# Prefix log-sum-exp on one core: the steps of a tile in another order, and the two-block tiles in other places

## The chip, the cores and the metric

The kernel runs on 1 core of one Trainium2 chip. The metric is the device time of one execution in microseconds, lower is better; the time of a kernel is the median of its runs. A separate, profiled execution left a trace: every instruction of every engine with its start and duration, and the transfers. Engine names in the profile: PE is TensorE (PEld its weight loads), DVE is VectorE, ACT is ScalarE, POOL is GpSimd, SP is SyncE, whose queue issues all of this kernel's transfers.

## The reference

```python
B, S, D = (4, 4096, 4128)           # x: float32, standard normal
out[:, 0, :] = x[:, 0, :].copy()
for t in range(1, S):
    mx = np.maximum(out[:, t - 1, :], x[:, t, :])
    out[:, t, :] = mx + np.log(np.exp(out[:, t - 1, :] - mx) + np.exp(x[:, t, :] - mx))
```

For each batch and column, row t of the output is the logarithm of the sum of exp(x) over rows 0 to t: a prefix sum between an Exp and a Ln.

## The kernel before, in words

**Tiles.** A batch has 4096 rows, 32 blocks of 128. A tile (`Step`) is r = 2 or 3 blocks: partition p of the tile holds r consecutive rows of all 4128 columns, so a tile is 128 x r x 4128 float32 (4128 KB or 6192 KB). A batch is cut into twelve tiles of [2, 3, 3, 3, 2, 3, 3, 3, 2, 3, 3, 2] blocks; four batches give 48 tiles (`steps`), 32 of three blocks and 16 of two. Four tile buffers rotate: one (`x2`) of two blocks, for tiles whose number in the batch divides by four, and three (`x3`) of three blocks. Exp, sums and Ln are done in place, so the output is stored from the buffer that the input was loaded into.

**Chunks.** The 4128 columns are cut into NC = 3 chunks of 1376 columns (`Chunk`). Each chunk of each tile goes through these steps:

- `exp` (L92, ScalarE): Exp of the chunk's r blocks, one instruction.
- `sums` (L94 to L107, VectorE): adds the r values of each partition. With r = 3, L103 puts block 0 + block 1 into block 1; L105 then writes the total into `z[c]`, on partitions 0 to 126 only. Partition 127 of `z[c]` still holds the running sum at the end of the previous tile, the carry.
- `head` (L113, TensorE): a product with a 128x128 matrix of ones and zeros gives, in a PSUM tile `pt` (two buffers), for each partition the sum of all earlier partitions and the carry (`carried`; in a batch's first tile `below`, without the carry). The profile shows six matmul records for each head.
- `add` (L117 to L130, VectorE): L121 adds `pt` to the first r - 1 blocks in place; L122 writes the sum of the last two blocks, the inclusive prefix at the partition's last row, into all of `z[c]`.
- `log` (L135 and L136, ScalarE): Ln of the first r - 1 blocks in place, and Ln of `z[c]` into the last block.

The next tile's L105 for the same chunk overwrites `z[c]`, so it must follow this L136.

**Probes.** The kernel takes Exp without subtracting a maximum. It records whether that was safe: the minimum over row 0 of a batch (L99, one partition, in `sums` of a batch's first tile) and the sum of `z` over the columns (L128, partitions 96 to 127, in `add` of a batch's last tile). At the end L188 to L202 turn these into a flag; if it is set, a slow general version runs (`_general`, not taken with these inputs).

**Order.** Nothing is scheduled by a planner: `manual_schedule()` leaves each engine with its instructions in the order in which the Python code writes them. The loop of before goes over all 144 chunks as one sequence, across tile borders. At chunk g it writes Exp of chunk g+2, sums of g+1, add of g, Ln of g, and then the head of g+1. With the last tile's chunks (`late`), Exp of g+2 and sums of g+1 come behind add and Ln of g.

**Transfers.** When the last chunk of a tile is done, SP gets the store of this tile i and behind it the load of tile i+3. That load goes into the buffer that tile i-1 used, so SP waits for the store of i-1 to have completed.

Of the kernel before, what the change touches and what calls it, by code (L numbers as in the profile page):

```python
# [10 lines left out]
ALU = mybir.AluOpType  # L11
AX = mybir.AxisListType
P = 128
MM = 512
NC = 3
# [5 lines left out]
def kernel(  # L21
# [5 lines left out]
    nc = tc.nc  # L27
    B, S, D = x.shape
# [16 lines left out]
        out=below, in_=below, pattern=[[1, P]], compare_op=ALU.is_ge,  # L45
# [5 lines left out]
        out=carried, in_=below, pattern=[[0, P]], compare_op=ALU.not_equal,  # L51
# [5 lines left out]
    probe = consts.tile([P, 2, B * NC], FP32, name="probe")  # L57
# [27 lines left out]
    class Chunk:  # L85
# [6 lines left out]
            nc.scalar.activation(e, e, ACT.Exp)  # L92

        def sums(self):  # L94
            t, r = self.t, self.t.r
            e = [t.xt[:, j, self.cols] for j in range(r)]
            if t.first:
                k = t.b * NC + self.c
                nc.vector.tensor_reduce(  # L99
                    out=probe[0:1, 1, k:k + 1], in_=e[0][0:1], op=ALU.min, axis=AX.X,  # L100
                )
            if r == 3:
                nc.vector.tensor_tensor(out=e[1], in0=e[0], in1=e[1], op=ALU.add)  # L103
            n = P - 1
            nc.vector.tensor_tensor(  # L105
                out=self.z[0:n], in0=e[r - 2][0:n], in1=e[r - 1][0:n], op=ALU.add,
            )  # L107
# [8 lines left out]

        def add(self):  # L117
            t, r = self.t, self.t.r
            e = t.xt[:, 0:r - 1, self.cols]
            base = self.pt.unsqueeze(1).to_broadcast([P, r - 1, CH])  # L120
            nc.vector.tensor_tensor(out=e, in0=base, in1=e, op=ALU.add)  # L121
            nc.vector.tensor_tensor(  # L122
                out=self.z, in0=t.xt[:, r - 2, self.cols], in1=t.xt[:, r - 1, self.cols],
                op=ALU.add,
            )
            if t.last:
                k = t.b * NC + self.c
                nc.vector.tensor_reduce(  # L128
                    out=probe[96:P, 0, k:k + 1], in_=self.z[96:P], op=ALU.add, axis=AX.X,
                )  # L130

        def log(self):
            t, r = self.t, self.t.r
            e = t.xt[:, 0:r - 1, self.cols]
            nc.scalar.activation(e, e, ACT.Ln)  # L135
            nc.scalar.activation(t.xt[:, r - 1, self.cols], self.z, ACT.Ln)  # L136

    steps = []
    for b in range(B):
        n = S // P  # L140
        parts = []
        while n:
            r = min(2 if len(parts) % 4 == 0 else 3, n)
            if n - r == 1:
                r = 2
            parts.append(r)
            n -= r
        assert len(parts) % 4 == 0 and min(parts) > 1
        row = 0
        for i, r in enumerate(parts):  # L150
            steps.append(Step(b, row, r, x3 if i % 4 else x2, i + 1 == len(parts)))
            row += P * r
        assert row == S

    chunks = [Chunk(s, c) for s in steps for c in range(NC)]
    bufs, ahead, stored = 4, 3, 0
    for s in steps[:bufs]:
        s.load()
    chunks[0].exp()
    chunks[1].exp()  # L160
    chunks[0].sums()
    chunks[0].head()
    n = len(chunks)
    for g, k in enumerate(chunks):
        nxt = chunks[g + 1] if g + 1 < n else None
        far = chunks[g + 2] if g + 2 < n else None
        late = far is None or far.t is steps[-1]
        if not late:
            far.exp()
            nxt.sums()  # L170
        k.add()
        k.log()
        if late:
            if far:
                far.exp()
            if nxt:
                nxt.sums()
        if k.c == NC - 1:
            k.t.store()
            if bufs <= stored + ahead < len(steps):  # L180
                steps[stored + ahead].load()
            stored += 1
        if nxt:
            nxt.head()


    bad = consts.tile([P, 2, B * NC], FP32, name="bad")
# [1 line left out]
        out=bad[:, 0, :], in0=probe[:, 0, :], scalar1=LARGE, scalar2=None, op0=ALU.is_le,  # L189
    )  # L190
    nc.vector.tensor_scalar(
        out=bad[:, 1, :], in0=probe[:, 1, :], scalar1=SMALL, scalar2=None, op0=ALU.is_ge,
# [3 lines left out]
        out=low, in_=bad.rearrange("p a k -> p (a k)"), op=ALU.min, axis=AX.X,  # L196
# [5 lines left out]
        out=flag, in0=good, scalar1=float(P), scalar2=None, op0=ALU.is_lt,  # L202
# [68 lines left out]
```

## Time and profile before

| | |
|---|---|
| median of 3 runs | 1296.87 us (1295.33 to 1296.93) |
| the profiled execution's own time | 1293.67 us |
| its span, first to last instruction | 1291.9 us |
| PE busy | 605.4 us, 47% |
| DVE busy | 996.0 us, 77% |
| ACT busy | 937.3 us, 73% |
| bytes moved | 541.28 MB, half read, half written |
| mean rate over the span | 419 GB/s |
| load of a three-block tile, issue to landing (median) | 38.9 us |
| store of a three-block tile, issue to landing (median) | 23.8 us |

How to read it: the shares of busy time are means over the whole span. The page also gives the span in 40 equal slices, one digit each (9 is 90% or more busy). A row of instructions says start, duration, engine, line, operation, output <- input with shapes, and in brackets the idle time ahead of it and what ended that. On one engine an instruction may start shortly before the listed end of the one in front of it, so "start to start" is the measure of what an instruction takes out of an engine's time.

### The profile page before, as it was taken

The page shows a single profiled execution, that of the slowest core. Times are in us where ns is not written, and L with a number is a line of the kernel's source. Part 1 is how long each engine was busy: PE and PEld are TensorE (multiplying, and loading weights), DVE is VectorE, ACT ScalarE, POOL GpSimd, SP SyncE. Part 2 cuts the span into 40 slices and gives each one's busy share as a digit, 9 for nine tenths or more (in the row PEclk, how much of TensorE's full clock was granted, in tenths as well). Part 3 has the DMA queues.
Part 4 walks back from the last instruction along what each step waited for, and adds up shares of the span by engine and source line. Part 5 has one row for each costly group of instructions (what it writes and reads, how often), then busy time and mean ns, then how long its engine had stood idle before and what let it go on. Part 6 is the DMA issues. An engine that isn't in the chain of part 4 may idle for free. (4 is left out here: it accounts for less than half of the span.)

```text
span 1291.9 us, 3364 instructions
## 1 busy us (share of the span) xinstructions
PE 605.4 (47%) x866; PEld 236.8 (18%) x866; DVE 996.0 (77%) x556; ACT 937.3 (73%) x433; POOL 4.6 (0%) x12
## 2 busy tenths in 40 slices
PE   2554356345555335545534534535534553463432
PEld 1221122112122112112211211211211221121110
DVE  4996798679689579669968957957968976895763
ACT  4996687678589669569669957866858866895761
POOL 1000000000000000000000000000000000000000
PEclk9766666667567667666766766766776666676566
DMA  9999999999999999999999999999999999999964
GB/s 402 423 413 428 433 429 432 436 430 404 438 433 427 439 427 431 435 430 420 423 425 435 439 428 439 428 438 426 415 429 429 435 434 432 434 437 429 433 279 180
DMA packets 13843, 541.28 MB, mean 419 GB/s; under 512 B 1536, under 2 KB 1536, under 8 KB 1536
## 3 DMA queue, kind: packets, MB, share of 16 engines
q1 hardware_dynamic: 13824, 541.07, 97.6%
q8 instruction: 7, 0.11, 0.0%
q14 instruction: 12, 0.10, 0.0%
HBM read 270.53 MB, written 270.53 MB: 419 GB/s over the span
## 5 line engine op out<-in xcount | busy, mean ns | idle before, releaser
L113 PE MATMUL pt<-z,carried 128*128 128x512 f32 (+1 forms) x792 | 557.9, 867 | 613.2 <-DVE z L105 613.2
L92 ACT ACTIVATE xt<-xt 128x4128 f32<-128x4128 f32 (+1 forms) x144 | 467.7, 3249 | 240.3 <-DMA xt<-in_x_dram 240.3
L113 PEld LDWEIGHTS pt<-z,carried 128*128 128x128 f32 x792 | 218.0, 293 | 952.4 <-issue 952.4
L121 DVE TENSOR_TENSOR xt<-pt,xt 128x2752 f32<-128x2752 f32 (+1 forms) x144 | 365.6, 2539 | 20.9 <-PE pt L113 20.9
L135 ACT ACTIVATE xt<-xt 128x2752 f32<-128x2752 f32 (+1 forms) x144 | 303.8, 2109 | 100.3 <-DVE z L122 99.7
L103 DVE TENSOR_TENSOR xt<-xt 128x1376 f32<-128x1376 f32 x96 | 152.3, 1587 | 216.4 <-ACT xt L92 216.3
L105 DVE TENSOR_TENSOR z<-xt 127x1376 f32<-127x1376 f32 x144 | 228.9, 1590 | 17.8 <-ACT xt L92 13.8
L122 DVE TENSOR_TENSOR z<-xt 128x1376 f32<-128x1376 f32 x144 | 229.3, 1593 | 4.9
L136 ACT ACTIVATE xt<-z 128x1376 f32<-128x1376 f32 x144 | 192.0, 1333 | 0.0
L113 PE MATMUL pt<-z,below 128*128 128x512 f32 (+1 forms) x72 | 47.3, 817 | 54.4 <-DVE z L105 54.4
L99 DVE TENSOR_REDUCE probe<-xt 1x1 f32<-1x1376 f32 x12 | 18.9, 1571 | 21.8 <-ACT xt L92 21.7
L113 PEld LDWEIGHTS pt<-z,below 128*128 128x128 f32 x72 | 18.7, 276 | 83.1 <-issue 82.9
L128 DVE TENSOR_REDUCE probe<-z 32x1 f32<-32x1376 f32 x12 | 19.0, 1581 | 0.4
L62 POOL MEMSET z<- 128x1376 f32 x3 | 3.7, 1245 | 0.0
L199 PE MATMUL good<-ones,low 128*1 128x1 f32 x2 | 0.2, 164 | 5.4 <-DVE low L195 5.4
L33 ACT ACT_TABLE_LOAD x1 | 1.3, 1283 | 0.8 <-PEq L255 0.8
L199 PEld LDWEIGHTS good<-ones,low 128*1 128x1 f32 x2 | 0.1, 82 | 6.0 <-DVE low L195 6.0
L201 DVE TENSOR_SCALAR flag<-good 1x1 int32<-1x1 f32 x1 | 0.1, 147 | 0.3 <-PE good L199 0.3
L44 POOL TENSOR_SCALAR_AFFINE_SELECT below<-below 128x128 f32<-128x128 f32 x1 | 0.3, 292 | 0.0
L50 POOL TENSOR_SCALAR_AFFINE_SELECT carried<-below 128x128 f32<-128x128 f32 x1 | 0.3, 292 | 0.0
L195 DVE TENSOR_REDUCE low<-bad 128x1 f32<-128x24 f32 x1 | 0.2, 179 | 0.0
L43 POOL MEMSET below<- 128x128 f32 x1 | 0.2, 204 | 0.3 <-POOLq L255 0.3
(8 smaller groups left out, 1.0 us busy)
## 6 DMA issues: line engine op xcount, KB each, us to landing
xt<-in_x_dram SPq DMA_DIRECT2D x32, 6192.0 KB, 38.9
out_dram<-xt SPq DMA_DIRECT2D x32, 6192.0 KB, 23.8
xt<-in_x_dram SPq DMA_DIRECT2D x16, 4128.0 KB, 33.2
out_dram<-xt SPq DMA_DIRECT2D x16, 4128.0 KB, 26.4
```

Of the source, the lines that this page charges most:

```text
L33: nc.scalar.preload_act_table_set("natural_log_exp_and_others")
L62: nc.gpsimd.memset(t, 0.0)
L92: nc.scalar.activation(e, e, ACT.Exp)
L99: nc.vector.tensor_reduce(out=probe[0:1, 1, k:k + 1], in_=e[0][0:1], op=ALU.min, axis=AX.X,)
L103: nc.vector.tensor_tensor(out=e[1], in0=e[0], in1=e[1], op=ALU.add)
L105: nc.vector.tensor_tensor(out=self.z[0:n], in0=e[r - 2][0:n], in1=e[r - 1][0:n], op=ALU.add,)
L113: nc.tensor.matmul(pt[:, a:b], lhsT=w, rhs=self.z[:, a:b], start=True, stop=True,)
L121: nc.vector.tensor_tensor(out=e, in0=base, in1=e, op=ALU.add)
L122: nc.vector.tensor_tensor(out=self.z, in0=t.xt[:, r - 2, self.cols], in1=t.xt[:, r - 1, self.cols], op=ALU.add,)
L128: nc.vector.tensor_reduce(out=probe[96:P, 0, k:k + 1], in_=self.z[96:P], op=ALU.add, axis=AX.X,)
L135: nc.scalar.activation(e, e, ACT.Ln)
L136: nc.scalar.activation(t.xt[:, r - 1, self.cols], self.z, ACT.Ln)
```

## The change

The loop now goes over tiles. Within a tile it writes: Exps of chunks 1 and 2 (the Exp of chunk 0 was written during the tile before), the sums of all three chunks, the heads of chunks 0 and 1, then for each chunk its add and its Lns, with the head of chunk 2 behind those of chunk 0. The next tile's first Exp is written ahead of add and Lns of chunk 2; with the last two tiles (`end`) it comes after the tile's last Ln. Store and load are written where they were, at the end of the tile, in the same order.

The min probe of a batch's first tile moves from `sums` to the start of `add`. In a batch's last tile, L122 and L128 become one instruction, `tensor_tensor_reduce`, which writes `z` and the sum of `z` over the columns, now on all 128 partitions.

The first three batches are cut into [2, 3, 3, 3, 2, 3, 2, 3, 2, 3, 3, 3] blocks; the last one stays as it was. The numbers of two- and three-block tiles stay the same, as do the buffers, the transfers' sizes and all of the arithmetic.

```diff
         def sums(self):
-            t, r = self.t, self.t.r
-            e = [t.xt[:, j, self.cols] for j in range(r)]
-            if t.first:
-                k = t.b * NC + self.c
-                nc.vector.tensor_reduce(
-                    out=probe[0:1, 1, k:k + 1], in_=e[0][0:1], op=ALU.min, axis=AX.X,
-                )
+            r = self.t.r
+            e = [self.t.xt[:, j, self.cols] for j in range(r)]
...
         def add(self):
             t, r = self.t, self.t.r
+            k = t.b * NC + self.c
+            if t.first:
+                nc.vector.tensor_reduce(
+                    out=probe[0:1, 1, k:k + 1], in_=t.xt[0:1, 0, self.cols],
+                    op=ALU.min, axis=AX.X,
+                )
             e = t.xt[:, 0:r - 1, self.cols]
             base = self.pt.unsqueeze(1).to_broadcast([P, r - 1, CH])
             nc.vector.tensor_tensor(out=e, in0=base, in1=e, op=ALU.add)
-            nc.vector.tensor_tensor(
-                out=self.z, in0=t.xt[:, r - 2, self.cols], in1=t.xt[:, r - 1, self.cols],
-                op=ALU.add,
-            )
+            ends = (t.xt[:, r - 2, self.cols], t.xt[:, r - 1, self.cols])
             if t.last:
-                k = t.b * NC + self.c
-                nc.vector.tensor_reduce(
-                    out=probe[96:P, 0, k:k + 1], in_=self.z[96:P], op=ALU.add, axis=AX.X,
+                nc.vector.tensor_tensor_reduce(
+                    out=self.z, in0=ends[0], in1=ends[1], scale=1.0, scalar=0.0,
+                    op0=ALU.add, op1=ALU.add, accum_out=probe[:, 0, k:k + 1],
                 )
+            else:
+                nc.vector.tensor_tensor(out=self.z, in0=ends[0], in1=ends[1], op=ALU.add)
...
+        parts = [2, 3, 3, 3, 2, 3, 3, 3, 2, 3, 3, 2] if b == B - 1 else \
+                [2, 3, 3, 3, 2, 3, 2, 3, 2, 3, 3, 3]
...
-    chunks[0].exp()
-    chunks[1].exp()
-    chunks[0].sums()
-    chunks[0].head()
-    n = len(chunks)
-    for g, k in enumerate(chunks):
-        nxt = chunks[g + 1] if g + 1 < n else None
-        far = chunks[g + 2] if g + 2 < n else None
-        late = far is None or far.t is steps[-1]
-        if not late:
-            far.exp()
-            nxt.sums()
-        k.add()
-        k.log()
-        if late:
-            if far:
-                far.exp()
-            if nxt:
-                nxt.sums()
-        if k.c == NC - 1:
-            k.t.store()
-            if bufs <= stored + ahead < len(steps):
-                steps[stored + ahead].load()
-            stored += 1
-        if nxt:
-            nxt.head()
+    for s in steps:
+        s.chunks = [Chunk(s, c) for c in range(NC)]
+    steps[0].chunks[0].exp()
+    for i, s in enumerate(steps):
+        k = s.chunks
+        end = i + 2 >= len(steps)
+        for c in range(1, NC):
+            k[c].exp()
+        for c in range(NC):
+            k[c].sums()
+        k[0].head()
+        k[1].head()
+        for c in range(NC):
+            if c == NC - 1 and not end:
+                steps[i + 1].chunks[0].exp()
+            k[c].add()
+            k[c].log()
+            if c + 2 < NC:
+                k[c + 2].head()
+        if end and i + 1 < len(steps):
+            steps[i + 1].chunks[0].exp()
+        s.store()
+        if bufs <= i + bufs - 1 < len(steps):
+            steps[i + bufs - 1].load()
```

More of the change, by code (lines that the diff above doesn't have):

```diff
@@ L139 @@
     for b in range(B):
[L140 to L148, printed above, removed]
+        parts = [2, 3, 3, 3, 2, 3, 3, 3, 2, 3, 3, 2] if b == B - 1 else \
+                [2, 3, 3, 3, 2, 3, 2, 3, 2, 3, 3, 3]
+        parts = parts[:len(parts) * S // (32 * P)] if S < 32 * P else parts
         row = 0
@@ L153 @@
         assert row == S
-    chunks = [Chunk(s, c) for s in steps for c in range(NC)]
-    bufs, ahead, stored = 4, 3, 0
+    bufs = 4
     for s in steps[:bufs]:
         s.load()
-    chunks[0].exp()
-    chunks[1].exp()
-    chunks[0].sums()
-    chunks[0].head()
-    n = len(chunks)
-    for g, k in enumerate(chunks):
-        nxt = chunks[g + 1] if g + 1 < n else None
-        far = chunks[g + 2] if g + 2 < n else None
-        late = far is None or far.t is steps[-1]
-        if not late:
-            far.exp()
-            nxt.sums()
-        k.add()
-        k.log()
-        if late:
-            if far:
-                far.exp()
-            if nxt:
-                nxt.sums()
-        if k.c == NC - 1:
-            k.t.store()
-            if bufs <= stored + ahead < len(steps):
-                steps[stored + ahead].load()
-            stored += 1
-        if nxt:
-            nxt.head()
+    for s in steps:
[22 more added lines that the diff above has]
+            steps[i + bufs - 1].load()
     bad = consts.tile([P, 2, B * NC], FP32, name="bad")
```

## The prediction

> **What bounds the kernel now.** I read the page first (busy shares, the DMA row, the queues), then the waits, then the windows of the end, and last the timelines of VectorE and ScalarE, from which the new order is priced.
>
> ```profile
> span 1291.9 us, 3364 instructions
> PE 605.4 (47%) x866; PEld 236.8 (18%) x866; DVE 996.0 (77%) x556; ACT 937.3 (73%) x433; POOL 4.6 (0%) x12
> ...
> DMA  9999999999999999999999999999999999999964
> ...
> q1 hardware_dynamic: 13824, 541.07, 97.6%
> ```
>
> No engine is above 77%, but the DMA row is full until the last two slices: 97.6% of 1291.9 is 1261 us for 541.1 MB, 429 GB/s. The waits (line, waited for, total, times, longest) agree: ScalarE waits for loads, and VectorE for what ScalarE gets late.
>
> ```profile
> ACT xt L92 <- DMA xt<-in_x_dram: 240.3, 40, 12.6
> DVE xt L103 <- ACT xt L92: 216.3, 29, 14.0
> ```
>
> So until the last loads land the transfers set the pace and compute has slack. Only the end is compute, with the transfers mostly idle (next-to-last column: DMA share):
>
> ```profile
> 1240.00:1250.00 10.00, 3.86 (x5) 1.83 (x6) 5.96 (x3) 5.42 (x3) 0.00 (x0) 0.50 0.19 79
> 1270.00:1280.00 10.00, 2.94 (x7) 1.00 (x6) 5.34 (x7) 2.59 (x2) 0.00 (x0) 0.67 0.12 53
> ```
>
> The seven windows 1220 to 1290 lack about 28 us of transfer. That is all that a better end could win; the rest can only be lost, if a tile's compute gets longer than its transfers. A three-block tile moves 2 x 6192 KB = 12.68 MB, 29.5 us at 429 GB/s; a two-block tile 19.7 us; a batch (8 and 4) 315 us.
>
> Compute of before, where it does not wait for loads (VectorE, then ScalarE, early in the run):
>
> ```profile
> 52.91 1.59 DVE L122 TENSOR_TENSOR z<-xt 128x1376 f32<-128x1376 f32 x1
> 54.42 1.58 DVE L103 TENSOR_TENSOR xt<-xt 128x1376 f32<-128x1376 f32 x1
> 56.04 1.59 DVE L105 TENSOR_TENSOR z<-xt 127x1376 f32<-127x1376 f32 x1
> 57.55 3.02 DVE L121 TENSOR_TENSOR xt<-pt,xt 128x2752 f32<-128x2752 f32 x1
> 60.60 1.59 DVE L122 TENSOR_TENSOR z<-xt 128x1376 f32<-128x1376 f32 x1
> ...
> 58.24 3.63 ACT L92 ACTIVATE xt<-xt 128x4128 f32<-128x4128 f32 x1
> 62.29 2.50 ACT L135 ACTIVATE xt<-xt 128x2752 f32<-128x2752 f32 x1 [0.42 <-DVE z L122]
> ```
>
> VectorE is gapless: start to start 1.51 (L122 to the next), 1.62 (L103 to L105, which needs it), 1.51 and 3.05, together 7.69 us a chunk, 23.1 us a three-block tile, under the 29.5 of its transfers. An Exp of one chunk and the sums of another run beside each other; that overlap is what the new order gives up. The Ln starts 0.10 us after L122 ends (60.60 + 1.59).
>
> ```profile
> 1166.09 1.59 DVE L122 TENSOR_TENSOR z<-xt 128x1376 f32<-128x1376 f32 x1
> ...
> 1178.02 3.64 ACT L92 ACTIVATE xt<-xt 128x4128 f32<-128x4128 f32 x1 [12.61 <-DMA xt<-in_x_dram]
> 1181.56 1.33 ACT L135 ACTIVATE xt<-xt 128x1376 f32<-128x1376 f32 x1
> 1181.69 1.59 DVE L103 TENSOR_TENSOR xt<-xt 128x1376 f32<-128x1376 f32 x1 [14.01 <-ACT xt L92]
> ```
>
> Here z was final at 1167.68, yet its Ln ran at 1181.56, after an Exp that waited for a load: ScalarE takes its instructions strictly in the written order. Exp to the next on ScalarE is 3.55 us, and L103 follows the Exp's end (1181.66) by 0.03.
>
> **The new order, priced for a three-block tile.** ScalarE's order becomes Exp 1, Exp 2, Ln 0, Ln 1, next tile's Exp 0, Ln 2; VectorE's is all sums, then all adds. Count from T, the start of Exp 1. Exp 2 starts at T+3.55 and reaches VectorE at T+7.21 (3.63 + 0.03). Sums of chunk 2: L103 1.62, L105 1.51, to T+10.34. Adds of chunk 0, which stand behind all sums in VectorE's queue: 3.05 + 1.51, to T+14.90. Add of chunk 1, to the start of its Ln: 3.05 + 1.59 + 0.10, T+19.64. Ln of chunk 1: 2.41 + 1.24 (L135 to L136, as 1195.82 to 1198.22, and L136 to the next), T+23.29. Next tile's Exp 0: 3.55, T+26.84. Ln 2: 3.65, T+30.49; there the next Exp 1 starts. One loop through ScalarE and VectorE, 30.49 us, in which each waits for the other; chunk 0's Ln and chunk 2's add lie beside it.
>
> Is another wait later? Chunk 0's heads start by T+0 at the latest; chunk 1's sums end at T+6.9 and its head (six matmuls, up to 4.93 us here, as in the row at 1246.14) at T+11.9; chunk 2's waits for L121 of chunk 0 to free its PSUM buffer (T+13.4) and ends at T+18.3, before its add is due at T+19.5. TensorE stays hidden by over a microsecond.
>
> **Two-block tile.** Exp to Exp is 2.40 (three in 7.27 us at 13.25), L135 and L121 have 1376 columns (1.25 and 1.61 to the next), and L103 is absent: 2.40 + 2.51 + 1.51 + (1.61 + 1.51) + (1.61 + 1.59 + 0.10) + 2.49 + next Exp 0 + 2.49 = 17.82 + next Exp 0. With each tile's Exp 0 counted to itself: 30.49 and 20.22 us. The head of chunk 1 ends at T+9.2 for an add due at T+9.5, so PE is covered by only 0.3 us here; half a microsecond more a head would cost some 3 us over the 16 such tiles.
>
> **Probes.** The min probes (L99, 1.50 to the next) move from the sums to ahead of the adds: in a batch's first tile two of three lie on the loop, 3.0 us a batch. L128 disappears as an instruction (1.60 x 12, mostly hidden before). The fused add and sum that replaces it and L122 is in no row. Below, it can cost what L122 costs, whose operands it has (nothing extra); above, L122 and L128 one after the other, 1.7 extra. Six of the twelve are on the loop (chunks 0 and 1 of three batches) and in the last tile about one more: 0 to 12 us. I take 0, since L122 is the nearest row, and keep 12 for the range. A rule speaks against this edit: the Trainium skill, "Vector Engine (DVE) Microarchitecture Reference", section "Points that are easy to get wrong", says that a two-input instruction with an accumulator runs at half rate on two SBUF sources that are not bf16. No run here shows it yet; by it the sum would grow by about 10 us.
>
> **Transfers.** Load i+3 is issued right behind store i: 29.5 us for both transfers and 3.4 around them (the last store takes 13.2 us for 9.8 us of bytes), so about 33 us later it has landed. Its first Exp is due two tiles on, less the Exp and Ln ahead of the store: 30.5 + 21.4 - 7.3 = 44.6 us in the tightest mix. Loads are early by some 11 us and ScalarE's wait for them goes away, as does the full DMA row. The load also waits on SP for store i-1 to be complete; that was issued a period (21 us at least) earlier and needs 18 alone; a few microseconds of delay here would still leave the load early. The new places of the two-block tiles change no sum here: the loop adds the same pieces in any order, and loads are not waited for. Grouping the Exps saves no table load, since the span has one (L33).
>
> **Sum.** First tile: Exp 0 at 13.25 as before, head 0 done at about 22.1, adds with probes 4.61 each to 31.4, Ln 1 2.5, next Exp 0 3.55, Ln 2 2.6: store 0 issued at 40.1 (41.83 before). Tiles 1 to 45: 31 x 30.49 + 14 x 20.22 + 3 x 3.0 = 1237.3. Tile 46 has no foreign Exp before its Ln 2, which then waits for add 2 (T+24.1): 27.9. Tile 47 starts cold: three Exps, then three heads in a row of 4.5 to 4.9 with add and Ln of the last: 24. From the last store to the end of the span as now (1291.9 - 1278.7): 13.2. Together 1342.5 span, against 1291.9. The profiled execution lies 1.8 above its span (1293.67), and the median of the runs 3.2 above that (1296.87): 1344.3 to 1347.5. I take 1346.
>
> **Rivals.** *The transfers stay the bound (faster).* If the loop were shorter than the transfers, 315 us a batch instead of 327.8 (243.9 + 80.9 + 3.0), load waits would stay and only the end would move: store 45 would follow load 46's landing (1207.25) by 7.3 us instead of 15.3, then 27.9 + 24 + 13.2 give 1279.6, 12.3 less: 1284.6. It decides if the loop loses 4%, 1.1 us a tile, for instance if an Exp could pass a waiting Ln. For it: 97.6% of DMA. Against it: the row at 1181.56, and every term of the loop is read from a row. 5%.
>
> *The fused instruction is dear.* Seven places at 1.4 to 1.7 us: 1356 to 1358. By the rule above, about 1356. Against it: the nearest row. 20%.
>
> *The order written is not the order run.* If the queues kept something like today's order, nothing beyond today's 1296.87. The trace of before runs exactly in its written order; 2%.
>
> **Numbers.** Forecast 73%: 1346, own range 1338 to 1351 (a tenth of a microsecond a tile on the handovers is 5 us; TensorE 3). The range, 1337 to 1362, adds the fused instruction's upper end. About 0.2% is what a measurement of this kernel can tell from no change. Faster 5%, within it 2%, slower 93%.
>
> **What would show it.** Right: DMA share near 94% and spread over the run; ScalarE's wait for loads nearly gone; in its place L135 and L103 waiting for each other's engine, 30.5 us between stores of three-block tiles and 21.4 behind a two-block one; store 0 near 40, store 47 near 1329. Wrong: stores 29.5 us apart with L92 still waiting for loads; or the fused row well above 1.6 us; or heads (L113) ending later than the adds are due.

## The result, and the profile after

The changed kernel takes 1340.81 us (median of 4 runs, 1340.53 to 1340.92), the kernel before 1296.48 us beside it: ratio 1.0343, 95% interval 1.0325 to 1.0361. The predicted time was 1346.0, in a range of 1337 to 1362.

The page of the changed kernel; in it L92 is still the Exp, L98 and L100 are the sums, L108 the head, L122 and L130 the add, L125 the fused add and sum, L116 the min probe, L135 and L136 the Lns:

```profile
span 1339.0 us, 3339 instructions
...
PE 553.0 (41%) x866; PEld 218.3 (16%) x866; DVE 984.6 (74%) x556; ACT 933.1 (70%) x433; POOL 4.6 (0%) x12
...
q1 hardware_dynamic: 13824, 541.07, 95.9%
...
L125 DVE CUSTOM_DVE_ANT_0 z<-xt 128x1376 f32<-128x1376 f32 x12 | 19.1, 1592 | 0.4
```

ScalarE and VectorE do as much as before (933 and 985 us against 937 and 996), in a span that is 47 us longer. The packets' time still adds up to 95.9% of the span, so the DMA share alone would look like a kernel bound by its transfers. The waits (waiter, waited for, total, times, longest) say otherwise:

```profile
ACT xt L135 <- DVE z L130: 348.4, 89, 7.9
DVE xt L98 <- ACT xt L92: 207.6, 96, 3.9
...
DVE z L100 <- ACT xt L92: 121.9, 48, 15.8
...
ACT xt L92 <- DMA xt<-in_x_dram: 11.2, 1, 11.2
```

Before, ScalarE waited 240 us in 40 places for loads. Now it waits for a load once, the very first, and the two compute engines wait for each other: ScalarE's Lns for VectorE's adds, VectorE's sums for ScalarE's Exps. One tile of the loop, first ScalarE, then VectorE:

```profile
101.28 7.16 ACT L92 ACTIVATE xt<-xt 128x4128 f32<-128x4128 f32 x2
116.35 2.50 ACT L135 ACTIVATE xt<-xt 128x2752 f32<-128x2752 f32 x1 [7.91 <-DVE z L130]
118.75 1.33 ACT L136 ACTIVATE xt<-z 128x1376 f32<-128x1376 f32 x1
120.91 2.50 ACT L135 ACTIVATE xt<-xt 128x2752 f32<-128x2752 f32 x1 [0.82 <-DVE z L130]
...
108.47 1.59 DVE L98 TENSOR_TENSOR xt<-xt 128x1376 f32<-128x1376 f32 x1 [0.32 <-ACT xt L92]
110.10 1.59 DVE L100 TENSOR_TENSOR z<-xt 127x1376 f32<-127x1376 f32 x1
111.61 3.02 DVE L122 TENSOR_TENSOR xt<-pt,xt 128x2752 f32<-128x2752 f32 x1
114.66 1.59 DVE L130 TENSOR_TENSOR z<-xt 128x1376 f32<-128x1376 f32 x1
116.17 3.02 DVE L122 TENSOR_TENSOR xt<-pt,xt 128x2752 f32<-128x2752 f32 x1
119.22 1.59 DVE L130 TENSOR_TENSOR z<-xt 128x1376 f32<-128x1376 f32 x1
```

With T = 101.28, Exps 1 and 2 end at T+7.16, the last sums start at T+7.19, add 0 at T+10.33, add 1 at T+14.89, and Ln 1 at T+19.63; the prediction had T+7.21, T+10.34, T+14.90 and T+19.64. The row with 7.91 us of idle time is ScalarE with nothing left to do: its next Exp is written behind these Lns. The stores, on SP's queue, show the period (29.3 us, with a two-block tile next, and 21.3):

```profile
101.40 0.33 SPq L83 DMA_DIRECT2D out_dram<-xt  x1
...
130.68 0.33 SPq L83 DMA_DIRECT2D out_dram<-xt  x1
...
152.02 0.33 SPq L83 DMA_DIRECT2D out_dram<-xt  x1
```

### The profile page after: what moved, and what is told of

The parts are those of the page before. It is cut to its first block, busy times and chain, and to the rows that moved or that the text cites. A ratio compares the mean times of both kernels' runs of the same rounds, so it can differ in the third digit from the quotient of the medians.

```text
span 1339.0 us, 3339 instructions
## 1 busy us (share of the span) xinstructions
PE 553.0 (41%) x866; PEld 218.3 (16%) x866; DVE 984.6 (74%) x556; ACT 933.1 (70%) x433; POOL 4.6 (0%) x12
## 3 DMA queue, kind: packets, MB, share of 16 engines
q1 hardware_dynamic: 13824, 541.07, 95.9%
## 5 line engine op out<-in xcount | busy, mean ns | idle before, releaser
L108 PE MATMUL pt<-z,carried 128*128 128x512 f32 (+1 forms) x792 | 508.1, 798 | 706.0 <-DVE z L100 604.6
L135 ACT ACTIVATE xt<-xt 128x2752 f32<-128x2752 f32 (+1 forms) x144 | 303.7, 2109 | 380.7 <-DVE z L130 348.4
L92 ACT ACTIVATE xt<-xt 128x4128 f32<-128x4128 f32 (+1 forms) x144 | 462.6, 3245 | 11.2 <-DMA xt<-in_x_dram 11.2
L122 DVE TENSOR_TENSOR xt<-pt,xt 128x2752 f32<-128x2752 f32 (+1 forms) x144 | 365.7, 2539 | 1.3
L108 PEld LDWEIGHTS pt<-z,carried 128*128 128x128 f32 x792 | 200.5, 270 | 1014.1 <-issue 883.5
L100 DVE TENSOR_TENSOR z<-xt 127x1376 f32<-127x1376 f32 x144 | 229.2, 1592 | 125.2 <-ACT xt L92 121.9
L98 DVE TENSOR_TENSOR xt<-xt 128x1376 f32<-128x1376 f32 x96 | 152.8, 1592 | 207.6 <-ACT xt L92 207.6
L130 DVE TENSOR_TENSOR z<-xt 128x1376 f32<-128x1376 f32 x132 | 210.1, 1592 | 4.5
L136 ACT ACTIVATE xt<-z 128x1376 f32<-128x1376 f32 x144 | 192.0, 1333 | 0.0
L108 PE MATMUL pt<-z,below 128*128 128x512 f32 (+1 forms) x72 | 44.7, 777 | 59.4 <-DVE z L100 51.8
L108 PEld LDWEIGHTS pt<-z,below 128*128 128x128 f32 x72 | 17.7, 260 | 85.3 <-issue 76.5
L125 DVE CUSTOM_DVE_ANT_0 z<-xt 128x1376 f32<-128x1376 f32 x12 | 19.1, 1592 | 0.4
L116 DVE TENSOR_REDUCE probe<-xt 1x1 f32<-1x1376 f32 x12 | 18.8, 1567 | 0.0
L125 DVE DVE_READ_ACCUMULATOR2_ANT probe<- 128x1 f32 x12 | 1.0, 82 | 0.0
```

The lines of the kernel that those rows point to most:

```text
L100: nc.vector.tensor_tensor(out=self.z[0:n], in0=e[r - 2][0:n], in1=e[r - 1][0:n], op=ALU.add,)
L108: nc.tensor.matmul(pt[:, a:b], lhsT=w, rhs=self.z[:, a:b], start=True, stop=True,)
L116: nc.vector.tensor_reduce(out=probe[0:1, 1, k:k + 1], in_=t.xt[0:1, 0, self.cols], op=ALU.min, axis=AX.X,)
L125: nc.vector.tensor_tensor_reduce(out=self.z, in0=ends[0], in1=ends[1], scale=1.0, scalar=0.0, op0=ALU.add, op1=ALU.add, accum_out=probe[:, ...
L130: nc.vector.tensor_tensor(out=self.z, in0=ends[0], in1=ends[1], op=ALU.add)
```

## The experiments

Each time is compared with the kernel before, run beside it (1296.06 us for the first four runs, 1294.28 in a single run for the next four, 1296.68 for the last three), or where said with the changed kernel's 1340.8.

**Where the next tile's first Exp stands.** One line of the changed kernel decides what ScalarE's queue holds ahead of the next tile's first Exp: Lns 0 and 1 (the changed kernel), Ln 0 alone, or no Ln.

```diff
-            if c == NC - 1 and not end:
+            if c == 1 and not end:
                 steps[i + 1].chunks[0].exp()
```

> The next tile's first Exp is written ahead of add and Lns of chunk 1 instead of chunk 2; nothing else differs from the changed kernel. Loop theory (the time is one closed loop through ScalarE and VectorE, and only what stands on it counts): the loop now leaves VectorE after chunk 0's add. Ln 0 starts at T+15.08, then Ln 0 3.65, Exp 3.55, Ln 1 3.65, Ln 2 3.65: 29.58 us a three-block tile instead of 30.49, and about 19.6 instead of 20.2 for a two-block tile. A batch is then about 316 us, level with the 315 us of its transfers: 1298 to 1303 us, some 40 less than the changed kernel. Grouping theory (doing all Exps, sums and products of a tile together costs the time, wherever the next Exp stands): within 5 us of 1341. Rest theory (the cost is in the tile sizes, the fused instruction or the probes): 1341.

Measured: 1299.78 us, 1.0028 of before (1.0013 to 1.0043). Two stores of this run, a three-block tile apart, and its wait for loads:

```profile
274.94 0.33 SPq L83 DMA_DIRECT2D out_dram<-xt  x1
...
304.43 0.33 SPq L83 DMA_DIRECT2D out_dram<-xt  x1
...
ACT xt L92 <- DMA xt<-in_x_dram: 11.8, 2, 11.1
```

The period is 29.49 us, where the loop sum had said 29.58 and the changed kernel has 30.42 at the same tile. Loads are waited for only twice, 11.8 us in all, so this time is still the shorter loop and not yet the transfers.

```diff
-            if c == NC - 1 and not end:
+            if c == 0 and not end:
                 steps[i + 1].chunks[0].exp()
```

> The next tile's first Exp is written ahead of add and Lns of chunk 0, so it runs while VectorE does the last sums. Loop theory: the loop is Exp 1, Exp 2, sums 2, adds 0 to 2, Ln 2: 27.85 us a three-block tile, under the 29.5 us of its transfers, so the transfers are the bound again and ScalarE waits for loads: 1289 to 1297 us, within 0.5% of the kernel before. Grouping theory: within 5 us of 1341. Rest theory: 1341.

Measured: 1292.0 us, 0.9966 of before (0.9952 to 0.9979). Both runs lie in the range expected; the grouping theory and the rest theory had 1341. The instructions, their number and all tile sizes are the changed kernel's; only one Exp a tile moved, ahead of one or two more pairs of Lns on ScalarE, and 41 or 49 us went. The second kernel's ScalarE and stores, its waits, and an earlier place in it (VectorE, then ScalarE):

```profile
725.02 9.55 ACT L92 ACTIVATE xt<-xt 128x4128 f32<-128x4128 f32 x3
740.09 2.50 ACT L135 ACTIVATE xt<-xt 128x2752 f32<-128x2752 f32 x1 [5.52 <-DVE z L130]
...
725.14 0.33 SPq L83 DMA_DIRECT2D out_dram<-xt  x1
...
752.97 0.33 SPq L83 DMA_DIRECT2D out_dram<-xt  x1
...
ACT xt L92 <- DMA xt<-in_x_dram: 217.4, 36, 11.8
...
492.55 1.59 DVE L130 TENSOR_TENSOR z<-xt 128x1376 f32<-128x1376 f32 x1
...
495.31 3.64 ACT L92 ACTIVATE xt<-xt 128x4128 f32<-128x4128 f32 x1 [5.92 <-DMA xt<-in_x_dram]
498.86 1.33 ACT L135 ACTIVATE xt<-xt 128x1376 f32<-128x1376 f32 x1
```

Three Exps now run in a row, the third in the hole that was 7.9 us; two stores with no load wait between them are 27.83 us apart, where the loop sum had said 27.85; that is less than the transfers' 29.5, and ScalarE waits for loads again, 217 us in all. An Exp that waits for a load still holds the Lns behind it: z was final at 494.14 and its Ln ran at 498.86. The Trainium skill, "Perfetto Trace Analysis", section "Tensor Engine Instruction (MATMUL, LD_WEIGHTS)", says that ScalarE and VectorE execute strictly first in, first out; this Ln, 4.72 us behind its z and directly behind the Exp, agrees.

**All of the change but its order.** The changed kernel with the loop over chunks of the kernel before: what stays are the new places of the two-block tiles, the fused instruction and the moved min probes.

```diff
-    for i, s in enumerate(steps):
-        k = s.chunks
...
+    for g, k in enumerate(chunks):
+        nxt = chunks[g + 1] if g + 1 < n else None
+        far = chunks[g + 2] if g + 2 < n else None
...
```

> The order of the kernel before with all else of the change: the new places of the two-block tiles, the fused instruction, the moved min probes. Loop theory: the transfers stay the bound, so these parts show only at the end, where the three sums of z are gone from the last tile's chain: 1290 to 1297 us. Rest theory: 1341, or most of the way there.

Measured: 1286.81 us, 0.9936 of before (0.9919 to 0.9952). The rest theory falls: the order alone costs the time, and the rest even gains some 9 us. My expectation, 1290 to 1297, was missed too, on the low side: it had looked for a gain only at the end of the run.

**The two-block tiles in the new order.** The changed kernel with [2, 3, 3, 3, 2, 3, 3, 3, 2, 3, 3, 2] in all batches:

> The changed kernel with the tile sizes of the kernel before in all four batches. Loop theory: the loop adds the same pieces in any order and loads are early (by about 6 us in the tightest place instead of 12): 1339 to 1343 us, the same as the changed kernel. Rival (the two-block tiles' places matter to the transfers): with two two-block tiles in a row a load comes late and ScalarE waits for it, over 1345 us.

Measured: 1340.6 us, the same as 1340.8. Here, where the compute loop is the bound, the places of the two-block tiles do nothing.

**Fewer bytes.** Both kernels store only the first row of each partition's two or three.

```diff
-            nc.sync.dma_start(out=self.dram(out), in_=self.xt)
+            nc.sync.dma_start(out=self.dram(out)[:, 0:1, :], in_=self.xt[:, 0:1, :])
```

> The changed kernel, which stores only the first of each partition's two or three rows, so that the output lacks the others: stores move a third (three-block tiles) or a half (two-block) of their bytes, 31% less in all. Loop theory: the transfers are not the bound, so only the last store gets shorter: 1334 to 1338 us. Transfer theory (the new order is slower because it feeds the transfers worse): at least 150 us less.

> The same cut of the stores in the kernel before. The transfers are its bound, so they get out of the way until the gapless VectorE of 23.1 us a three-block tile and some 18 to 20 us a two-block tile is the bound: 1060 to 1090 us, over 200 less. If compute were its bound already: within 10 us of 1296.

Measured in one run each: 1335.4 us for the new order, 5.4 less than the changed kernel, and 1072.5 us for the old one, 222 less than the 1294.28 beside it; both lie in the ranges expected. Of the 5.4 us, 4.8 lie behind the last store's issue (8.4 us to the end of the span instead of 13.2). The page of the old order:

```profile
PE 596.3 (56%) x866; PEld 232.4 (22%) x866; DVE 993.9 (93%) x556; ACT 935.4 (87%) x433; POOL 4.6 (0%) x12
```

With 31% fewer bytes the old order drives VectorE to 93%: that is the room that it had and that the new order gave up. The new order, but for its last store, does not notice the missing bytes.

**The same instruction on and off the loop.** One more VectorE instruction in each tile but the first of a batch, for c = 0 or for c = 2:

```diff
             if t.first:
                 nc.vector.tensor_reduce(
                     out=probe[0:1, 1, k:k + 1], in_=t.xt[0:1, 0, self.cols],
                     op=ALU.min, axis=AX.X,
                 )
+            elif self.c == 0:
+                nc.vector.tensor_reduce(
+                    out=spare[0:1, 0:1], in_=t.xt[0:1, 0, self.cols], op=ALU.min, axis=AX.X,
+                )
```

> The changed kernel with one more VectorE instruction in each tile but a batch's first: the min over one partition of chunk 0, ahead of add 0 (1.66 us start to start, as in the rows of the first tiles). Loop theory: it stands on the loop, 43 times 1.66 and a little at the end: 71 us more, 1411 us. Throughput theory (VectorE is busy 74% and has room): under 10 us more.

> The same extra instruction ahead of add 2. Add 2 ends at T+24.1, 2.7 us before its Ln may start behind the next tile's Exp (1.6 us where the next tile has two blocks), so 1.66 us fits: only the last two tiles, whose Ln 2 waits for add 2, pay. Loop theory: 3 to 6 us more, 1343 to 1347 us. If VectorE's time counted wherever it stands: 71 us more.

Measured in one run each: 1414.6 us ahead of add 0, 73.8 more than the changed kernel (44 times 1.66 is 73.0; I had counted 43 times and 71), and 1348.1 us ahead of add 2, 7.3 more, which misses the expected 3 to 6 by a microsecond. Ahead of add 0 every tile that has the instruction takes about 1.7 us longer; two stores a three-block tile apart, 32.12 us instead of 30.42:

```profile
298.76 0.33 SPq L84 DMA_DIRECT2D out_dram<-xt  x1
...
330.88 0.33 SPq L84 DMA_DIRECT2D out_dram<-xt  x1
```

Ahead of add 2 the row is

```profile
717.59 1.57 DVE L122 TENSOR_REDUCE spare<-xt 1x1 f32<-1x1376 f32 x1
719.25 3.02 DVE L127 TENSOR_TENSOR xt<-pt,xt 128x2752 f32<-128x2752 f32 x1
```

(the extra lines shift the line numbers), 1.66 us start to start as on the loop. The stores show where the 7.3 lie: 3.7 up to store 45, all of it 0.2 to 0.7 us at each of 14 tiles ahead of a two-block tile, where the cover of 1.6 us is not quite enough, and 3.6 in the last two tiles. The same 44 instructions cost ten times more in one place than in the other, with VectorE idle a quarter of the time.

**What gained in the rest.** The miss of the third run was taken apart: the kernel before with only the new tile sizes, and the old order and sizes with only the fused instruction and the moved probes.

> The kernel before with only the new places of the two-block tiles in the first three batches. The run with the old order and all the rest of the change took 1286.8 us, some 9 less than the kernel before, where no more than 5 had been expected from the fused instruction at the end. Parts theory: two two-block tiles in a row at a batch's border let the transfers slow down (428, 425 and 427 GB/s in the windows 300:400, 600:700 and 900:1000 of before, 433, 433 and 434 in that run: 2 MB less moved, 4.7 us at 430 GB/s), so this run gives 1290 to 1293 us. If the parts do nothing: 1295 to 1297, and all 9 us belong to the fused instruction and the probes.

> The old order and the old tile sizes with only the fused instruction and the moved min probes. In the chain that ended last before, three L128 of 1.60 us stand between the last tile's adds and the next sums or Lns: without them 3 to 5 us less, 1291 to 1293 us. If the fused instruction also explains the transfers at the batch borders: 1287.

Measured: 1288.53 us, 0.9935 of before (0.9918 to 0.9952), for the tile sizes alone, and 1293.9 us, 0.9977 (0.9966 to 0.9988), for the fused instruction alone; the first gains 8.2 us, more than the 4 to 7 expected, the second 2.8, slightly less than the 3 to 5 expected. Together that is 11, where the run with both gained 9; the intervals, about 2 us either way, allow it. Windows at the three batch borders, the new sizes and then the kernel before (last columns: TensorE clock, DMA share, GB/s):

```profile
250.00:300.00 50.00, 22.21 (x30) 8.35 (x30) 40.94 (x22) 42.51 (x18) 0.00 (x0) 0.66 1.00 433
600.00:650.00 50.00, 23.26 (x35) 8.76 (x33) 44.08 (x26) 35.56 (x18) 0.00 (x0) 0.67 1.00 432
900.00:950.00 50.00, 25.76 (x35) 10.49 (x36) 48.22 (x27) 39.31 (x19) 0.00 (x0) 0.68 1.00 433
```

```profile
250.00:300.00 50.00, 22.58 (x34) 8.98 (x35) 41.43 (x23) 38.14 (x18) 0.00 (x0) 0.72 0.99 417
600.00:650.00 50.00, 29.03 (x42) 11.23 (x42) 43.03 (x26) 32.63 (x19) 0.00 (x0) 0.73 0.99 414
900.00:950.00 50.00, 28.39 (x42) 11.13 (x40) 47.51 (x28) 42.29 (x22) 0.00 (x0) 0.73 1.01 423
```

Where two two-block tiles follow each other, the same 16 DMA engines, just as full, move 414 to 423 GB/s instead of 432 or 433; the run with the old sizes and the fused instruction has 428, 413 and 420 in these windows. Over three times 50 us the difference is worth some 5 us, and the last load of the profiled execution is issued 5.4 us earlier with the new sizes (1187.3 instead of 1192.7). So most of the difference between these two executions comes from the borders; the medians lie 8 apart. That the tile sizes cause it is shown; why the packets are slower there is not.

**A version that beats both.** The old order with the rest of the change, the last tile kept in the same order as all others, and stored chunk by chunk:

```diff
-        late = far is None or far.t is steps[-1]
+        late = far is None
...
+        if k.t is steps[-1]:
+            nc.sync.dma_start(out=k.t.dram(out)[:, :, k.cols], in_=k.t.xt[:, :, k.cols])
         if k.c == NC - 1:
-            k.t.store()
+            if k.t is not steps[-1]:
+                k.t.store()
```

> A version made to beat both: the old order with all the rest of the change; the last tile's Exps and sums keep the same place as all others (no late case), so that heads and Exps of the last two tiles overlap (chunk after chunk at 6.1 to 7.7 us, as at 97 to 115 us in the kernel before, instead of 9.6 to 11); and the last tile is stored chunk by chunk, so that only a third of its 9.8 us of bytes is left behind the last Ln. Loop and transfer theory: 12 and 6 us less than 1286.8: 1266 to 1272 us. If something else holds the end (the flag, the loads of the last tile): over 1280.

Measured: 1270.12 us, 0.9799 of before (0.978 to 0.9818), in the range expected. The two parts were not run apart, but the profiled executions show both. Against the run with the old order and the rest of the change, the last store is issued 11.5 us earlier (1258.4 instead of 1269.9), and the span ends 10.0 us behind it instead of 13.3; 12 and 6 had been expected. The last two slices, where the kernel before had 279 and 180 GB/s:

```profile
GB/s 408 418 400 441 425 431 431 432 439 432 428 433 432 431 434 432 435 430 435 431 438 433 433 428 438 426 439 434 427 433 436 433 433 436 433 431 429 433 362 334
```

## Why the prediction was right

- **The loop** was the right mechanism and the right size: 30.49 us predicted for a three-block tile, 30.42 measured (stores at 70.98 and 101.40), 21.37 and 21.34 for a two-block one. Store 45 was due at 40.1 + 1237.3 = 1277.4 and was issued at 1276.9. The runs with the Exp elsewhere and with the extra instruction show that it is this loop: with the Exp ahead of add 1 the loop holds Ln 0 in place of add 1, and the three-block period falls by 0.93 us (0.91 summed); with the Exp ahead of add 0 it holds add 2 in place of Ln 1 and the Exp, and falls by 2.6 (2.64 summed); and an instruction of 1.66 us put on the loop lengthens each tile by 1.7, where off it the same instruction costs nothing at most tiles.
- **The first rival** (the transfers stay the bound) had its deciding point right, a batch's loop against its 315 us. From the first store of one batch to that of the next (batches 2 and 3), the changed kernel takes 327.6 to 327.9 us (327.8 predicted), the run with the Exp ahead of add 1 takes 316.9, and the one with the Exp ahead of add 0, whose loop is shorter than its transfers, 315.2 to 316.1.
- **The second rival** (the fused instruction is dear) is out: its row has 1592 ns, what L122 of before had, and its read of the sum (0.08 us) runs beside the next instruction. By the Trainium skill's rule of half rate ("Vector Engine (DVE) Microarchitecture Reference", section "Points that are easy to get wrong") it would have been about 3.2 us, an estimate from twice L122's 1.59. The page states the rule for one instruction layout, S2S2D2_STT, and no trace here shows whether the fused instruction has that layout; the 1592 ns decide, and this instruction does not pay the price.
- **The third** (the order written is not the order run) is out by the same timelines.
- **Off in size: the min probes.** They were counted at 1.50 us each, 3.0 a batch. In their new place they take 1.66 start to start (349.71 to 351.37), and the first tile of a later batch takes 3.4 to 3.6 us longer than other two-block tiles. That is 1.3 us too little in all; 31 three-block tiles at 0.07 us less than summed outweigh it.
- **Off in size: tile 47.** The term was 24 us with three heads in a row of 4.5 to 4.9 each; it took 21.1, because only the first head took long:

```profile
1313.58 1.59 DVE L122 TENSOR_TENSOR xt<-pt,xt 128x1376 f32<-128x1376 f32 x1
...
1316.72 1.58 DVE L122 TENSOR_TENSOR xt<-pt,xt 128x1376 f32<-128x1376 f32 x1
...
1319.86 1.58 DVE L122 TENSOR_TENSOR xt<-pt,xt 128x1376 f32<-128x1376 f32 x1
```

  The first head begins at 1308.86, 4.7 us ahead of the first of these adds; then the adds follow each other at VectorE's own 3.14 us. In the window 1310 to 1320 the granted clock was 0.84, where in the windows of before from 1230 to 1280 it was 0.50 to 0.67; why it was higher, and whether it made the heads short, was not tried. The tile is 2.9 of the 3.5 us by which the span came in under 1342.5. The other 1.7 us of the 5.2 are the runs: the median of the changed kernel lies on its profiled execution (1340.73), where before it lay above.
- **The places of the two-block tiles** were said to change no sum. That was said of the new order and holds there (1340.6 with the old ones). It would be wrong for the kernel before, where they are worth 8 us: there loads are waited for, and the rate of the transfers is not the same everywhere.
- **DMA share**: 94% was said, 95.9% measured.

## What to carry to other kernels

Write out the closed loop of an order across in-order engines, one pass of it with start-to-start times from the trace of the old order, and compare it with what the transfers need for the same tile: busy shares (74% and 70% here) say nothing on it. Where an instruction can run early, put it into the hole where its engine waits for the other one, not behind the instruction that ends that hole; here that place was worth 49 us for one line. And what is worth nothing under one bound can be worth something under the other (the tile sizes, 0 and 8 us), so undo such parts one by one before they go with a change that lost.

## What the hardware showed that was not expected

In this kernel the transfer rate of a full queue depends on the tile sequence: 413 to 428 GB/s at the batch borders of the two runs with two two-block tiles in a row, against 429 to 433 in the same windows of the two runs with the new sizes, at a DMA share of 0.99 to 1.01 in all of them. A two-input add that also sums its output costs 1592 ns on 1376 float32 columns, the same as without the sum. And the last tile's three heads in a row met a granted clock of 0.84, where the single heads at the end of before met 0.50 to 0.67.
